# Three weight tiles at a time at the start of each inner sub-layer, and the last norm on VectorE alone

## The chip, the cores and the metric

The kernel runs on one core of one Trainium2 chip. The metric is device time in microseconds (us) of one execution. TensorE (PE) multiplies, VectorE (DVE) and ScalarE (ACT) work on its inputs and results, GpSimd (POOL) does a few adds and issues some DMAs, and SyncE (SP) issues nearly all DMAs.

## What is computed

Two layers, each a mixer sub-layer and an MLP sub-layer, on 16 meta tokens and 512 tokens of 1024 features, all in float32. Each sub-layer normalises its input and its output (`rmsnorm` divides by the root of the mean square over the 1024 features):

```python
for l in range(DEPTH):
    a = rmsnorm(h, mix_pre_g[l])
    proj = a @ w_in[l]
    ...
    y = jnp.concatenate([rmsnorm(y_attn, attn_out_g[l]),
                         rmsnorm(y_conv, conv_out_g[l])], axis=-1)
    h = h + rmsnorm(y @ w_out[l], mix_post_g[l])
    a = rmsnorm(h, mlp_pre_g[l])
    f = jnp.square(jax.nn.relu(a @ w_up[l])) @ w_down[l]
    h = h + rmsnorm(f, mlp_post_g[l])
return h[:, N_META:]
```

`proj` holds the queries, keys and values of a windowed attention with rotary positions, and three inputs of a gated convolution.

## The kernel before

**Layout.** Activations lie transposed: 128 features (a k tile, 8 in all) on the partitions, tokens along the row. The 528 tokens are worked in two halves, A of 272 (or 256, `XA`, in the second layer where the meta tokens are no longer needed) and B of 256 tokens. A float32 product is three matmuls (`mm3`, L193 to L195): weight and activation are split into a high and a low part (`whi`, `wlo`, `a_hi`, `a_lo`), and the product of the low parts is left out. So one output tile (128 features) of one half is 8 k tiles by 3, 24 matmuls, in a PSUM bank.

**Weights** come in half tiles over SP's queue. ScalarE makes `whi` (L108) and VectorE `wlo` (L109), up to `CAP` = 7 tiles ahead.

**A boundary** (`boundary`) ends a sub-layer and starts the next. TensorE multiplies the last 6 output tiles of half B while `Post` for half A (`pA`) runs beside it, k tile by k tile (`step`): `t = z * s` (L321, or L323 with a gain), `h += t` (L324), both on VectorE; `a_hi` (L330) and a square (L276) on ScalarE; the sum of squares `acc` (L277) and, one k tile later, `a_lo` (L335) on VectorE. `s` is the reciprocal root of the mean square of `z`: TensorE adds up over the partitions (`meansq`, L232), ScalarE takes three steps (L242 to L244) and VectorE two (L245, L246). Below, that is "the chain".

**`first_tiles`** then runs the first 5 output tiles (`NA`) of the next sub-layer on half A, one after another, each with its own loop over k; `mms`, which it calls, can run several items side by side, with all their matmuls of one k tile before the next. After k = 1 of the first tile, the call `pB.start` issues the mean square of half B, and between the tiles `pB.steps` issues the steps of half B, two k tiles each. In tile 2, after k = 5, stands `rstd_a`, the mean square of half A for the next norm. Then tiles 0 to 2 run side by side on half B (72 matmuls), and tiles 3 and 4. Evacuations of the results and low parts (L904, L281) run on VectorE, with ScalarE between. At the start of the kernel the same function is called with `Start` in the place of `Post` (`initial`).

There are three inner boundaries: from the first mixer to the first MLP (B0), from the first MLP to the second mixer (B1) and from the second mixer to the second MLP (B2). In B1 the five first tiles are v, k and three of q. v is scaled by its rstd (L576) and transposed on TensorE (L582); k and q are rotated on VectorE (L558 to L560, L602, L612), with DMAs that swap rows.

**The last norm** (`finish`, L342 to L359) has no next sub-layer: per k tile of 256 tokens a multiply by `s`, an add to `h`, and a store of 128 KB. Six k tiles run on VectorE with stores from SP's queue, two (`LAST_ON_POOL`) on GpSimd with stores from ScalarE's queue.

**Order.** A scheduler that replays the program on a model of the engines fixes each engine's order; the code gives only the order of issue and the data that must wait.

## Time and profile before

| | |
|---|---|
| time, median of 3 runs | 1141.37 us (1140.63 to 1142.13) |
| the profiled execution, time | 1140.6 us |
| its span | 1138.8 us |
| PE busy | 1088.9 us, 96% |
| DVE busy | 822.3 us, 72% |
| ACT busy | 641.2 us, 56% |
| POOL busy | 20.2 us, 2% |
| granted TensorE clock, mean | 0.975 of full speed |
| chain of work that ended last | PE 87%, DVE 7%, ACT 3% |
| PE idle until DVE's `acc` (L277), before L232 | 20.9 us, 9 times |
| PE idle until ACT's `a_hi` (L330) | 6.2 us |
| PE idle until DVE's `a_lo` (L335) | 4.1 us |

Busy time is the time in which an engine had an instruction in work. A PE that is busy is not one at its peak: its matmuls overlap, and their spacing, not their duration, is what one costs. The span is from the first to the last event of the trace; the execution's own time is 1.8 us more.

### The profile page before, as it was taken

How to read it: one execution, taken by the hardware profiler on the slowest of the kernel's cores; microseconds unless marked ns; L12 is line 12 of the kernel's file. 1: busy time of each engine (PE TensorE's matmuls, PEld its weight loads, DVE VectorE, ACT ScalarE, POOL GpSimd, SP SyncE). 2: the span in 40 equal slices, each digit the busy share in tenths (PEclk: the TensorE clock that was granted, in tenths of full speed). 3: DMA queues.
4: the chain of work that ended last, by engine and by line, in shares of the span. 5: the costliest groups of instructions: out<-in, count | busy, mean ns of one | idle time of the engine just before them, and what ended most of it. 6: DMA issues, size and time to landing. Idle time of an engine off the chain costs nothing.

```text
span 1138.8 us, 21453 instructions
## 1 busy us (share of the span) xinstructions
PE 1088.9 (96%) x8066; PEld 1042.9 (92%) x8066; DVE 822.3 (72%) x1941; ACT 641.2 (56%) x1542; POOL 20.2 (2%) x56
## 2 busy tenths in 40 slices
PE   8999889899999999999989997898999999999995
PEld 8999789899999999999978997898888988988995
DVE  7987867868486586586689878678855856856836
ACT  8665766655383274275456556666734734724732
POOL 3000000000000000000000000000000000000001
PEclk9999989899999999999989999898999999999998
DMA  9242122242243243144132421222422522522502
GB/s 263 66 124 65 38 75 68 81 117 70 66 131 102 61 126 112 50 119 130 43 88 59 116 63 47 66 75 75 123 81 65 148 85 65 156 77 67 147 1 75
DMA packets 197672, 102.04 MB, mean 90 GB/s; under 512 B 7424, under 2 KB 197520, under 8 KB 197568
## 3 DMA queue, kind: packets, MB, share of 16 engines
q1 hardware_dynamic: 196960, 100.15, 30.4%
q8 instruction: 63, 1.03, 0.4%
q14 instruction: 41, 0.34, 0.1%
q10 hardware_dynamic: 432, 0.32, 0.1%
q0 software_dynamic: 176, 0.21, 0.1%
HBM read 97.88 MB, written 2.10 MB: 88 GB/s over the span
## 4 chain that ended last, share of the span: by engine, by line
PE 87%; DVE 7%; ACT 3%; issue 1%; DMA 1%; SPq 0%; DVEq 0%; POOL 0%; ACTq 0%
PE ps L195 28%; PE ps L193 28%; PE ps L194 27%; PE ps L199 2%; DVE wlo L109 1%; PE ps L232 1%; ACT S L647 1%; DMA h<-in_xT 1%; DVE acc L277 1%; PE ps L693 1%; DVE p L281 1%; DVE a_lo L335 0%; DVE S L658 0%; DVE z L706 0%; DVE h L324 0%
## 5 line engine op out<-in xcount | busy, mean ns | idle before, releaser
L194 PE MATMUL ps<-f_lo,whi 128*128 128x256 f32 (+2 forms) x1072 | 326.1, 305 | 0.0
L195 PE MATMUL ps<-f_hi,wlo 128*128 128x256 f32 (+2 forms) x1072 | 325.4, 305 | 0.0
L193 PE MATMUL ps<-f_hi,whi 128*128 128x256 f32 (+2 forms) x1072 | 323.7, 306 | 0.0
L193 PE MATMUL ps<-a_hi,whi 128*128 128x256 f32 (+3 forms) x808 | 242.5, 302 | 7.2 <-ACT a_hi L330 6.2
L194 PE MATMUL ps<-a_lo,whi 128*128 128x256 f32 (+3 forms) x808 | 238.5, 295 | 4.6 <-DVE a_lo L335 4.1
L195 PE MATMUL ps<-a_hi,wlo 128*128 128x256 f32 (+3 forms) x808 | 237.1, 294 | 0.3 <-DVE wlo L109 0.3
L194 PEld LDWEIGHTS ps<-f_lo,whi 128*128 128x128 f32 x1072 | 201.7, 188 | 9.6
L195 PEld LDWEIGHTS ps<-f_hi,wlo 128*128 128x128 f32 x1072 | 201.9, 189 | 9.2
L193 PEld LDWEIGHTS ps<-f_hi,whi 128*128 128x128 f32 x1072 | 200.1, 188 | 9.3
L108 ACT ACTIVATE whi<-wraw 128x512 fp32r<-128x512 f32 x264 | 153.8, 623 | 94.2 <-PE ps L194 65.6
L109 DVE TENSOR_TENSOR wlo<-wraw,whi 128x512 fp32r<-128x512 f32 x264 | 173.1, 686 | 44.0 <-ACT whi L108 21.3
L193 PEld LDWEIGHTS ps<-a_hi,whi 128*128 128x128 f32 x808 | 157.7, 196 | 11.9 <-ACT a_hi L330 8.2
L194 PEld LDWEIGHTS ps<-a_lo,whi 128*128 128x128 f32 x808 | 158.2, 196 | 9.3 <-DVE a_lo L335 6.5
L195 PEld LDWEIGHTS ps<-a_hi,wlo 128*128 128x128 f32 x808 | 158.5, 196 | 1.8 <-DVE wlo L109 0.5
L505 DVE TENSOR_TENSOR z<-z,ps 128x272 f32<-128x272 f32 (+2 forms) x78 | 37.9, 486 | 100.3 <-PE ps L195 100.2
L194 PE MATMUL ps<-a_lo,wf 128*128 128x264 f32 (+1 forms) x384 | 108.0, 283 | 0.0
L193 PE MATMUL ps<-a_hi,wf 128*128 128x264 f32 (+1 forms) x384 | 107.8, 283 | 0.0
L108 ACT ACTIVATE wf<-wraw 128x512 fp32r<-128x512 f32 x96 | 59.7, 626 | 84.3 <-PE ps L194 51.5
L195 PE MATMUL ps<-a_hi,wf 128*128 128x264 f32 (+1 forms) x384 | 107.1, 283 | 0.0
L108 ACT ACTIVATE wf<-u 128x512 fp32r<-128x512 f32 x72 | 45.2, 628 | 87.8 <-PE ps L194 73.6
L109 DVE TENSOR_TENSOR wf<-wraw,wf 128x512 fp32r<-128x512 f32 x96 | 65.5, 686 | 10.9 <-ACT wf L108 9.8
L194 PEld LDWEIGHTS ps<-a_lo,wf 128*128 128x128 f32 x384 | 72.2, 188 | 0.1
(179 smaller groups left out, 1833.9 us busy)
## 6 DMA issues: line engine op xcount, KB each, us to landing
wraw<-in_w_up SPq DMA_DIRECT2D x128, 256.0 KB
wraw<-in_w_down SPq DMA_DIRECT2D x128, 256.0 KB
wraw<-in_w_in SPq DMA_DIRECT2D x72, 256.0 KB
wraw<-in_w_out SPq DMA_DIRECT2D x32, 128.0 KB
wraw<-in_w_out SPq DMA_DIRECT2D x16, 256.0 KB
outT<-h SPq DMA_DIRECT2D x14, 128.0 KB
h<-in_xT SPq DMA_DIRECT2D x4, 272.0 KB
h<-in_xT SPq DMA_DIRECT2D x4, 256.0 KB
```

The lines of the kernel that those rows point to most:

```text
L108: ACT.activation(hi, raw, AF.Copy)
L109: DVE.tensor_tensor(lo, raw, hi.bitcast(F32), ALU.subtract)
L193: PE.matmul(ps, whi, ahi, start=first, stop=False, skip_group_check=onto)
L194: PE.matmul(ps, whi, alo, start=False, stop=False, skip_group_check=onto)
L195: PE.matmul(ps, wlo, ahi, start=False, stop=last, skip_group_check=onto)
L199: PE.matmul(ps, a[n], b[n], start=first and n == 0, stop=last and n == 1)
L232: PE.matmul(ps, ones[:, which, :], acc, start=True, stop=more is None)
L277: return (eng or DVE).tensor_tensor(acc, acc, sq, ALU.add)
L281: DVE.tensor_tensor(lo, src, hi.bitcast(F32), ALU.subtract)
L505: DVE.tensor_tensor(zz, zz, ps, ALU.add)
L647: ACT.activation(S[:, i, keys], S[:, i, keys], AF.Exp, bias=ng[:, i:i + 1], accum_out=dn[:, i:i + 1])
L693: PE.transpose(bk[:, j * P:(j + 1) * P], S[:, j, kb * P:(kb + 1) * P], ident)
```

## The change

In `first_tiles` the first three tiles of half A are now one call of `mms` (side by side), where the sub-layer is an inner one. `pB.start` stands after k = 4 of the group, `rstd_a` after k = 5 of tile 3, and two `pB.steps` follow the group. `finish` uses VectorE only, with instructions over two k tiles and four stores of 256 KB, by turns from SP and ScalarE. The sums of squares of the start (`Start.sums`) use VectorE only, too, and the tile whose issue the five small DMAs of GpSimd wait for (`self.pool`) is another; in the built order these DMAs stand first of GpSimd's work.

```diff
-LAST_ON_POOL = (3, 6)
...
         def finish(self):
 
             t0, t1 = self.r
+            n = t1 - t0
             self.start()
-            for eng, ks, queue in ((DVE, [k for k in range(KT) if k not in LAST_ON_POOL], nc.sync), (POOL, LAST_ON_POOL, nc.scalar)):
...
+            both = self.s.unsqueeze(1).to_broadcast([P, 2, n])
+            for k in range(0, KT, 2):
+                t = utile()[:, :2 * n].rearrange("p (k t) -> p k t", k=2)
+                hk = h[:, k:k + 2, t0:t1]
+                DVE.tensor_tensor(t, z[:, k:k + 2, t0:t1], both, ALU.mult)
+                DVE.tensor_tensor(hk, hk, t, ALU.add)
+                (nc.sync, nc.scalar)[k // 2 % 2].dma_start(
+                    outT.rearrange("(k p) t -> p k t", p=P)[:, k:k + 2, t0 - NM:t1 - NM], hk)
...
-                s = add_sq("h", k == 0, h[:, k, self.r[0]:self.r[1]], self.r, DVE if k % 2 else POOL)
-                self.pool = s if k == 2 else self.pool
+                s = add_sq("h", k == 0, h[:, k, self.r[0]:self.r[1]], self.r)
+                self.pool = s if k == 3 else self.pool
...
         initial = isinstance(pB, Start)
-        at = (2, 4) if initial else (2, 5)
-        for i in range(NA):
+        at = (2, 4) if initial else (3, 5)
+        groups = [(i,) for i in range(NA)] if initial else [(0, 1, 2), (3,), (4,)]
+        steps = iter(range(4))
+        for group in groups:
+            i = group[0]
             hooks = {}
             if i == 0:
-                hooks = {1: pB.start}
+                hooks = {1 if initial else 4: pB.start}
             if i == at[0]:
                 hooks = {at[1]: rstd_a}
             if not initial:
-                evs += mms([iA[i]], act, hooks)
+                evs += mms([iA[j] for j in group], act, hooks)
...
+            ready = [evs] if initial else [evs[:3]] if i == at[0] else [[ev] for ev in evs]
             if i >= at[0]:
...
-            if i < 4:
-                pB.steps(i)
-            after(i)
+            for n in (0, 1)[:1 if len(group) == 1 else 2]:
+                m = next(steps, None)
+                if m is not None:
+                    pB.steps(m)
+            after(group[-1])
```

Line numbers shift: L193 to L195 become L192 to L194, L232 becomes L231, L324 L323 and L335 L334; behind `first_tiles` L558 becomes L560, L576 L578, L612 L614 and L904 L906.

TensorE at B0, before: the end of tile 0 on half A (`ps_2936`), the mean square of half B (`acc_2244`), and the start of tile 1 (`ps_2985`).

```order
L195 MATMUL ps_2936<-a_hi_70,wlo_2562 128x272
L193 MATMUL ps_2936<-a_hi_70,whi_2561 128x272 [waits Activation_49]
L194 MATMUL ps_2936<-a_lo_71,whi_2561 128x272 [waits DVE_49]
L195 MATMUL ps_2936<-a_hi_70,wlo_2562 128x272
L232 MATMUL ps_2944<-acc_2244,ones_86 128x256 [waits DVE_49]
L193 MATMUL ps_2985<-a_hi_70,whi_2669 128x272
L194 MATMUL ps_2985<-a_lo_71,whi_2669 128x272
```

And now: the last k tile of the group (three banks, `ps_2936` to `ps_2938`), the mean square of half B, and the start of tile 3 (`ps_3051`).

```order
L192 MATMUL ps_2936<-a_hi_70,whi_2561 128x272 [waits Activation_49]
L192 MATMUL ps_2937<-a_hi_70,whi_2669 128x272
L192 MATMUL ps_2938<-a_hi_70,whi_2721 128x272
L193 MATMUL ps_2936<-a_lo_71,whi_2561 128x272 [waits DVE_49]
L194 MATMUL ps_2936<-a_hi_70,wlo_2562 128x272
L193 MATMUL ps_2937<-a_lo_71,whi_2669 128x272
L194 MATMUL ps_2937<-a_hi_70,wlo_2670 128x272
L193 MATMUL ps_2938<-a_lo_71,whi_2721 128x272
L194 MATMUL ps_2938<-a_hi_70,wlo_2722 128x272
L231 MATMUL ps_2985<-acc_2244,ones_86 128x256 [waits DVE_49]
L192 MATMUL ps_3051<-a_hi_70,whi_2776 128x272
```

The mean square of half B stood behind 24 matmuls of half A, each k tile's three waiting by themselves for that k tile; it now stands behind 72, nine to a k tile.

VectorE at B0, before: the end of half B's steps, with the evacuations (L904) and low parts (L281) of half A's tiles among them; the last `a_lo` is the third row from the end.

```order
L324 TENSOR_TENSOR h<-h,t 128x256 [waits DVE_49]
L281 TENSOR_TENSOR f_lo<-t,f_hi 128x272 [waits Activation_49]
L321 TENSOR_TENSOR t<-z,s 128x256
L335 SCALAR_TENSOR_TENSOR a_lo<-h,gt,a_hi 128x256 [waits Activation_49]
L324 TENSOR_TENSOR h<-h,t 128x256 [waits DVE_49]
L277 TENSOR_TENSOR acc<-acc,t 128x256 [waits Activation_49]
L904 TENSOR_SCALAR t<-ps 128x272 [waits PE_49]
L335 SCALAR_TENSOR_TENSOR a_lo<-h,gt,a_hi 128x256 [waits Activation_49]
L277 TENSOR_TENSOR acc<-acc,t 128x256 [waits DVE_49,Activation_49]
L281 TENSOR_TENSOR f_lo<-t,f_hi 128x272 [waits Activation_49]
```

And now; again the third row from the end.

```order
L323 TENSOR_TENSOR h<-h,t 128x256 [waits DVE_49]
L280 TENSOR_TENSOR f_lo<-t,f_hi 128x272 [waits Activation_49] x2
L320 TENSOR_TENSOR t<-z,s 128x256
L334 SCALAR_TENSOR_TENSOR a_lo<-h,gt,a_hi 128x256 [waits Activation_49]
L276 TENSOR_TENSOR acc<-acc,t 128x256 [waits Activation_49]
L323 TENSOR_TENSOR h<-h,t 128x256 [waits DVE_49]
L334 SCALAR_TENSOR_TENSOR a_lo<-h,gt,a_hi 128x256 [waits Activation_49]
L276 TENSOR_TENSOR acc<-acc,t 128x256 [waits Activation_49]
L906 TENSOR_SCALAR t<-ps 128x256 [waits PE_49] x3
```

Up to the last `h` (L324 before, L323 now) there stand, counted from the chain's end (L246, L245), one more `acc`, one more evacuation and one more `f_lo`, three rows; and the last `a_lo` follows its `h` at once, where an `acc` and an evacuation stood between them.

VectorE at B1, before: the rotations of q (L558, L559, L560, L612) around the last steps of half B; the last `a_lo` is the tenth row.

```order
L324 TENSOR_TENSOR h<-h,t 128x256 [waits DVE_49]
L559 TENSOR_TENSOR t<-t,z 128x256 [waits DMAHW2_49,DMAHW7_49,DMAHW1_49,DMAHW0_49]
L323 SCALAR_TENSOR_TENSOR t<-z,gt,s 128x256
L612 TENSOR_TENSOR f_hi<-t,f_hi 64x256 [waits Activation_49]
L612 TENSOR_TENSOR f_lo<-t,f_lo 64x256 [waits Activation_49]
L324 TENSOR_TENSOR h<-h,t 128x256 [waits DVE_49]
L335 SCALAR_TENSOR_TENSOR a_lo<-h,gt,a_hi 128x256 [waits Activation_49]
L277 TENSOR_TENSOR acc<-acc,t 128x256 [waits Activation_49]
L558 TENSOR_TENSOR t<-z 128x256
L335 SCALAR_TENSOR_TENSOR a_lo<-h,gt,a_hi 128x256 [waits Activation_49]
L277 TENSOR_TENSOR acc<-acc,t 128x256 [waits DVE_49,Activation_49]
```

And now; the last `a_lo` is the last row.

```order
L614 TENSOR_TENSOR f_hi<-t,f_hi 64x256 [waits Activation_49]
L614 TENSOR_TENSOR f_lo<-t,f_lo 64x256 [waits Activation_49]
L562 TENSOR_TENSOR t<-t 128x256 [waits DVE_49]
L323 TENSOR_TENSOR h<-h,t 128x256 [waits DVE_49]
L561 TENSOR_TENSOR t<-t,z 128x256 [waits DMAHW5_49,DMAHW6_49,DMAHW4_49,DMAHW3_49]
L322 SCALAR_TENSOR_TENSOR t<-z,gt,s 128x256
L614 TENSOR_TENSOR f_hi<-t,f_hi 64x256 [waits Activation_49]
L614 TENSOR_TENSOR f_lo<-t,f_lo 64x256 [waits Activation_49]
L334 SCALAR_TENSOR_TENSOR a_lo<-h,gt,a_hi 128x256 [waits Activation_49]
L323 TENSOR_TENSOR h<-h,t 128x256 [waits DVE_49]
L276 TENSOR_TENSOR acc<-acc,t 128x256 [waits Activation_49]
L334 SCALAR_TENSOR_TENSOR a_lo<-h,gt,a_hi 128x256 [waits Activation_49]
```

The rotation of one more query tile (L561, L614 twice) has moved ahead of the last two `a_lo`; the low part of v's transposes (`vv`, L281), which stood ahead of the k tile before these, has moved behind it.

## Rows read from the trace of the kernel before

**Rows 1.** The page, part 4: the share of the span that each engine holds of the chain of work that ended last.

```profile
PE 87%; DVE 7%; ACT 3%; issue 1%; DMA 1%; SPq 0%; DVEq 0%; POOL 0%; ACTq 0%
```

**Rows 2.** TensorE's timeline around the boundary from the first mixer to the first MLP: start (us), duration (us), engine, line, operation, tiles, shape, count, and in brackets the idle time before it and what ended it. The rows are the first matmul of the next sub-layer on half A, the last before its first wait, one of its waits, the mean-square matmuls of half B, the first matmul of the three tiles on half B, and the mean-square matmuls behind their 72.

```profile
203.69 0.29 PE L193 MATMUL ps<-a_hi,whi 128*128 128x272 f32 x1
...
205.82 0.29 PE L195 MATMUL ps<-a_hi,wlo 128*128 128x272 f32 x1
...
208.37 0.47 PE L194 MATMUL ps<-a_lo,whi 128*128 128x272 f32 x1 [1.11 <-DVE a_lo L335]
...
212.13 1.22 PE L232 MATMUL ps<-acc,ones 128*128 128x256 f32 x2 [1.14 <-DVE acc L277]
...
226.63 0.28 PE L193 MATMUL ps<-a_hi,whi 128*128 128x256 f32 x1
...
235.16 0.59 PE L232 MATMUL ps<-acc,ones 128*128 128x256 f32 x2
```

**Rows 3.** Busy time by stretches of 4 us of the same boundary: stretch, length, then for PE, PEld, DVE, ACT and POOL the busy us and the number of instructions that start in it; then TensorE's granted clock, the DMA share and GB/s.

```profile
204.00:208.00 4.00, 2.50 (x18) 2.07 (x17) 3.63 (x10) 3.13 (x8) 0.00 (x0) 1.00 0.25 72
...
208.00:212.00 4.00, 2.05 (x5) 1.16 (x5) 3.41 (x9) 2.95 (x7) 0.00 (x0) 0.57 0.43 127
...
212.00:216.00 4.00, 3.87 (x17) 3.69 (x18) 2.36 (x6) 1.55 (x4) 0.00 (x0) 0.58 0.89 256
```

**Rows 4.** VectorE's and (213.45) ScalarE's timeline at the same boundary, columns as in rows 2: the start of the chain of half B, two `wlo` subtractions in a row, then the `h` and the low part (`a_lo`) of its last k tile, and the first evacuation after them.

```profile
213.45 0.47 ACT L242 ACTIVATE t<-ps,epst 128x256 f32<-128x256 f32 x1 [1.21 <-PE ps L232]
...
211.99 1.29 DVE L109 TENSOR_TENSOR wlo<-wraw,whi 128x512 fp32r<-128x512 f32 x2
...
228.26 0.42 DVE L324 TENSOR_TENSOR h<-h,t 128x256 f32<-128x256 f32 x1
...
229.28 0.48 DVE L335 SCALAR_TENSOR_TENSOR a_lo<-h,gt,a_hi 128x256 fp32r<-128x256 f32 x1
...
234.65 0.78 DVE L904 TENSOR_SCALAR t<-ps 128x256 f32<-128x256 f32 x2 [3.86 <-PE ps L195]
```

**Rows 5.** The boundary from the first MLP to the second mixer: TensorE's timeline (mean square of half B, the transposes of v, the mean square behind the 72 matmuls on half B), VectorE's timeline (the mixer's rstd of half A, the evacuation of v, the low part of v's transposes, the `h` of the last k tile of half B), and two stretches of busy time as in rows 3.

```profile
579.39 1.22 PE L232 MATMUL ps<-acc,ones 128*128 128x256 f32 x2 [1.15 <-DVE acc L277]
...
594.01 0.49 PE L582 MATMUL ps<-ident,u 128*128 128x128 f32 x3
...
606.64 1.06 PE L232 MATMUL ps<-acc,ones 128*128 128x256 f32 x2
...
590.03 0.44 DVE L245 SCALAR_TENSOR_TENSOR t<-ps,t 128x272 f32<-128x272 f32 x1 [0.39 <-ACT t L244]
...
592.17 0.43 DVE L576 TENSOR_TENSOR u<-ps,rt 128x272 f32<-128x272 f32 x1
...
595.07 0.56 DVE L281 TENSOR_TENSOR vv<-ps,vv 128x384 fp32r<-128x384 f32 x1 [1.40 <-ACT vv L280]
...
602.94 0.43 DVE L324 TENSOR_TENSOR h<-h,t 128x256 f32<-128x256 f32 x1
...
598.00:602.00 4.00, 2.90 (x25) 2.69 (x23) 3.90 (x10) 2.16 (x6) 0.35 (x2) 1.00 0.16 41
...
602.00:606.00 4.00, 2.81 (x15) 2.60 (x16) 3.41 (x10) 1.94 (x6) 0.00 (x0) 0.81 0.01 2
```

**Rows 6.** The boundary from the second mixer to the second MLP: TensorE (first matmul on half A, mean square of half B, mean square behind the 72 on half B), ScalarE (start of the chain of half B), VectorE (an evacuation that waits, and the `h` of the last k tile of half B).

```profile
772.11 0.28 PE L193 MATMUL ps<-a_hi,whi 128*128 128x256 f32 x1
...
780.39 1.22 PE L232 MATMUL ps<-acc,ones 128*128 128x256 f32 x2 [1.27 <-DVE acc L277]
...
803.53 0.59 PE L232 MATMUL ps<-acc,ones 128*128 128x256 f32 x2
...
781.71 0.47 ACT L242 ACTIVATE t<-ps,epst 128x256 f32<-128x256 f32 x1 [1.21 <-PE ps L232]
...
789.52 0.42 DVE L904 TENSOR_SCALAR t<-ps 128x256 f32<-128x256 f32 x1 [0.19 <-PE ps L195]
...
796.47 0.42 DVE L324 TENSOR_TENSOR h<-h,t 128x256 f32<-128x256 f32 x1
```

**Rows 7.** The last norm: TensorE's mean-square matmuls, ScalarE's first step after them, then VectorE's multiplies (L354) and adds (L358) and GpSimd's multiplies.

```profile
1126.68 0.70 PE L234 MATMUL ps<-t,ones 128*128 128x256 f32 x2 [0.53 <-ACT t L508]
...
1127.42 0.47 ACT L242 ACTIVATE t<-ps,epst 128x256 f32<-128x256 f32 x1 [0.25 <-PE ps L234]
...
1129.74 1.29 DVE L354 TENSOR_TENSOR t<-z,s 128x256 f32<-128x256 f32 x2
...
1130.95 0.94 DVE L358 TENSOR_TENSOR h<-h,t 128x256 f32<-128x256 f32 x1
...
1133.54 0.41 DVE L354 TENSOR_TENSOR t<-z,s 128x256 f32<-128x256 f32 x1
...
1135.21 0.75 DVE L358 TENSOR_TENSOR h<-h,t 128x256 f32<-128x256 f32 x2
...
1129.84 1.76 POOL L354 TENSOR_TENSOR t<-z,s 128x256 f32<-128x256 f32 x2 [469.98 <-DVE s L246]
```

**Rows 8.** The start of the kernel: from the list of waits of the first 40 us (engine, line, what it waits for: us in all, times, longest), one stretch of busy time as in rows 3, and GpSimd's first DMA issue.

```profile
DVE acc L277 <- POOL acc L277: 1.3, 2, 0.7
...
8.00:12.00 4.00, 3.26 (x14) 2.52 (x15) 3.15 (x6) 4.00 (x11) 3.04 (x5) 0.82 1.16 325
...
9.69 0.71 POOL L1035 DMA_DIRECT2D ident<-in_ident  x1
```

More of the change, by code (lines that the diff above doesn't have):

```diff
@@ L344, in finish @@
             t0, t1 = self.r
+            n = t1 - t0
             self.start()
-            for eng, ks, queue in ((DVE, [k for k in range(KT) if k not in LAST_ON_POOL], nc.sync), (POOL, LAST_ON_POOL, nc.scalar)):
-                last, ts = None, {}
-                for n in range(len(ks) + 1):
-                    with ExitStack() as es:
-                        if last is not None:
-                            es.enter_context(tc.issue_after(last.ins))
-                        if n < len(ks):
-                            ts[n] = tmp(t1 - t0)
-                            last = eng.tensor_tensor(ts[n], z[:, ks[n], t0:t1], self.s, ALU.mult)
-                    if n:
-                        k = ks[n - 1]
-                        with tc.issue_after(last.ins):
-                            last = eng.tensor_tensor(h[:, k, t0:t1], h[:, k, t0:t1], ts[n - 1], ALU.add)
-                        self.store(queue, k)
+            both = self.s.unsqueeze(1).to_broadcast([P, 2, n])
[6 more added lines that the diff above has]
+                    outT.rearrange("(k p) t -> p k t", p=P)[:, k:k + 2, t0 - NM:t1 - NM], hk)
         def flush(self):
@@ L443, in first_tiles @@
                 evs += mms([iA[i]], act, hooks)
+            ready = [evs] if initial else [evs[:3]] if i == at[0] else [[ev] for ev in evs]
             if i >= at[0]:
-                waiting = pend[:]
-                pend.clear()
-                for ev in evs:
-                    ev()
-                evs = []
-                for f in waiting:
-                    f()
-            if i < 4:
-                pB.steps(i)
-            after(i)
+                for run in ready:
+                    waiting = pend[:]
+                    pend.clear()
+                    for ev in run:
+                        ev()
+                    for f in waiting:
+                        f()
+                evs = [] if initial else evs[3:] if i == at[0] else []
+            for n in (0, 1)[:1 if len(group) == 1 else 2]:
[3 more added lines that the diff above has]
+            after(group[-1])
         cap[0] = pcap
```

## The prediction

> **What bounds the kernel now.** I read the chain of work that ended last first: PE holds 87% of it [rows 1]. So a change pays where TensorE waits or runs at its lower clock, and at the two ends, where TensorE is not the last. Next I read TensorE's timeline at the inner boundaries. At B0 the first matmul on half A starts at 203.69 and the next ones follow 0.125 us apart (17 steps to 205.82); then tile 0 waits for k tiles 6 and 7, for a high or a low part each time, 1.11 us in the row shown, and the mean square of half B starts only at 212.13, after 1.14 us for the sum of squares [rows 2]. The stretches say what that costs twice over: the granted clock is 1.00 in 204 to 208 and 0.57 and 0.58 (between the levels of 2.4 and 1.2 GHz) in 208 to 216, where 17 matmuls take 3.87 us, 0.228 each [rows 3]. Behind it TensorE runs through: the 72 matmuls of tiles 0 to 2 on half B go from 226.63 to 235.16, 0.118 each, with no wait. VectorE meanwhile is ahead: the last low part of half B starts at 229.28, and then VectorE has nothing to do for 3.86 us [rows 4]. B2 is the same picture, B1 is not: there VectorE has rotations to do, the low parts come last, and TensorE stands at 602 to 606 (15 matmuls in 4 us) [rows 5].
>
> **B0, step by step.** With three tiles side by side each k tile gives TensorE nine matmuls, 1.13 us, instead of three. Half A's last parts had all come by 210.99 (212.13 less the 1.14 of waiting), and the group needs k tile 7 after 63 matmuls, at 203.69 + 63 x 0.125 = 211.6. So the waits go, and with them the low clock. But the mean square of half B now stands behind 72 matmuls, 203.69 + 72 x 0.125 = 212.69. ScalarE's part of the chain started 1.32 us behind it at the lower clock (213.45) [rows 2, 4]; at the full clock the row of the last norm gives 0.74 (1126.68 to 1127.42) [rows 7]. 212.69 + 0.74 = 213.43: the chain starts when it started before.
>
> What is late next is therefore VectorE. From 214.85 to 230 it hardly paused before, so rows count. The new order puts three more rows ahead of the last `h`; a row costs 0.34 (the spacing of 1133.54 to 1135.21, five steps). So `h` comes at 228.26 + 3 x 0.335 = 229.26, and the last `a_lo` 1.02 behind it as before (228.26 to 229.28: ScalarE's `a_hi` lies between), done 0.48 later, at 230.76. Of half B's last nine matmuls six need it: 6 x 0.118 = 0.71. The mean square that stood at 235.16 stands at about 231.5: **3.7 us** gained. Behind these new waits on TensorE are only tiles 3 and 4 of half B, and their evacuations move forward with them. If the extra rows cost nothing it is 4.6; if ScalarE adds half a row to each of the last k tiles, 3.0.
>
> **B2.** 772.11 + 72 x 0.118 = 780.61, plus 0.74 is 781.35, where the chain started at 781.71: 0.36 earlier. An evacuation that waited 0.19 no longer does. The last `h`: 796.47 - 0.36 - 0.19 + 1.0 = 796.92; plus 1.02, 0.48 and 0.71 is 799.1, against 803.53 [rows 6]: **4.4 us**, between 3.7 and 5.4 for the same reasons.
>
> **B1.** The sum of squares decides the start of the chain (579.39) in both kernels; the full clock gives 0.58 (1.32 less 0.74). The rstd for v no longer waits 0.39, since the mean square of half A follows 18 matmuls behind. The 1.40 us for v's transposes go, because that row now stands behind eight others. Against this the new order puts six rows more ahead of the last `h`: one `a_lo`, three steps of rotation, two rotated halves of a query, about 2.3 us. The last `h` stays where it was: 602.94 - 0.58 - 0.39 - 1.40 + 2.3 = 602.9; with 1.02, 0.48 and six matmuls (0.71, or 1.4 at the lower clock) that ends at 605.1 to 605.8, against 606.64. TensorE itself gains nothing of its 5.8 us earlier end of half A: it waits for v's evacuation, now at about 591.2 (592.17 - 0.97), before the transposes [rows 5]. I take **0.8 us**, and -1.0 to 1.5 as bounds: the lower one if the rotation's DMAs or ScalarE hold the query that moved forward.
>
> **Last norm.** Before, six k tiles on VectorE and two on GpSimd. While GpSimd worked, one VectorE instruction of 256 took 0.94 us, alone 0.41, with 0.34 from start to start [rows 7]. Now eight instructions of 512. Their nearest row is the pair of `wlo` subtractions of that size: 1.29 for two, so 0.60 from start to start and 0.69 for the last [rows 4]. 1129.74 + 7 x 0.605 + 0.69 = 1134.66, against 1135.21 + 0.75 = 1135.96: 1.3 less. The last store is 256 KB instead of 128, at the 325 GB/s of row 8:12 0.4 us more [rows 8]. Together **0.85 us**; 0.3 if nothing overlaps between instructions (0.69 each), 1.3 if the store costs nothing.
> By the Trainium skill (VectorE: DVE Perf Modes, "The TRN2 errata") such an instruction pays a fixed cost each time and takes 691 ns at 512 elements; an estimate from that page is 8 x 0.691 = 5.5 us, and the sum would end 0.6 us later. The duration of the row agrees; the start of the next does not wait for it, so I keep the row.
>
> **Start.** Six adds of 0.34 us go from GpSimd to VectorE, 2.0 us, and the 1.3 us that VectorE waited for GpSimd's go away. The five small DMAs, which began at 9.69, now stand ahead of the big loads: 196 KB at 325 GB/s are 0.6 us if TensorE's first operands are behind them [rows 8]. Bounds 0.6 lost to 0.3 gained; I take **0.3 lost**, since the loads are what the start waits for.
>
> **Sum.** 3.7 + 4.4 + 0.8 + 0.85 - 0.3 = 9.45. The profiled execution took 1140.6 (its span of 1138.8 and 1.8 around it, which I leave as they are): 1131.15. It lies 0.77 under the median of 1141.37, so the forecast is **1131.9**.
>
> **Rivals.** *The clock falls in the new waits.* Half B's 72 matmuls now wait for each of the last four k tiles, about 0.7 us in 1.75. At B1 TensorE waits in the same manner: the stretch 598 to 602, busy for 2.90 of 4 us, kept a clock of 1.00, the next one, with the two longest waits, shows 0.81 [rows 5]. The new waits lie between. A fall costs what 17 matmuls lost in 212 to 216, 3.87 - 17 x 0.125 = 1.7 us [rows 3], at B0 and at B2: 1135.3.
>
> *TensorE is the bound, VectorE keeps up.* Then B0 ends at 203.69 + 120 x 0.125 + 0.5 + 72 x 0.118 = 227.7, 7.5 us gained, and B2 at 772.11 + 192 x 0.118 + 0.5 = 795.3, 8.2: 1124. Against it stands that VectorE hardly pauses there.
>
> *B1 pays* the lower bound: 1133.7.
>
> *Nothing comes of it:* the gain of half A is given back whole in half B's waits. About 1140.6 to 1141.4. That needs `h` some 4 us later than worked out.
>
> *Slower:* half B's chain now starts behind 72 matmuls. If the group ran at 0.228 each, it would take 16.4 us, end at 220.1 at B0, and the chain start at 221.4, 8.0 later than worked out, 8.5 at B2. The terms 3.7 and 4.4 become -4.3 and -4.1: 1148.4. It turns to a loss where the chain starts 4.7 us later at both, that is with 46 of the 72 at the lower clock. Against it: clock 1.00 in 204 to 208, and no wait left in the group.
>
> **How the numbers follow.** Forecast 0.50; clock 0.22; TensorE the bound 0.08; B1 pays 0.10; nothing 0.05; slower 0.05. All the better bounds together give 13.1 us (1128.3), all the worse ones 5.1 (1136.3). The range 1128 to 1136 takes in forecast, clock and B1, 0.82. Faster by over 0.2% (2.3 us, about what a measurement of this kernel can tell from no change) are the first four, 0.90; within it 0.05; slower 0.05.
>
> **What would show it.** Right: no wait in the 72 matmuls of half A, granted clock 1.00 in 204 to 216, mean square of half B near 212.7; waits for `a_lo` in half B's group, and the mean square behind it near 231.5 less what the start moved; B1 nearly unchanged in length, with TensorE idle some 6 us before v's transposes; eight instructions of 0.6 us at the end. Wrong: a clock under 1.00 behind 224 or 794, `a_lo` rows of half B without pauses and yet later, or a first real matmul over 0.6 us later than before.

## The result and the profile after

The changed kernel took 1130.86 us (median of 4 runs, 1129.28 to 1131.79), the kernel before 1141.0 (4 runs, 1140.44 to 1142.13): a ratio of 0.9903, interval 0.9884 to 0.9922. That is 10.1 us less; 9.45 was forecast. The profiled execution after is the quickest of its four (1129.28, span 1127.5), so the two traces lie 11.3 us apart.

The page, parts 2 and 4: the granted clock in 40 slices, and the shares of the chain that ended last. VectorE holds 8% of it, 7% before [rows 1]. The mean clock went from 0.975 to 0.983.

```profile
PEclk9999989999999999999999999899999999999998
...
PE 87%; DVE 8%; ACT 3%; issue 1%; DMA 1%; SPq 0%; DVEq 0%; ACTq 0%
```

**B0.** TensorE's timeline, columns as in [rows 2]: the first matmul on half A, the mean square of half B, the first of the 72 matmuls on half B, the waits among them, the mean square behind them.

```profile
202.94 0.29 PE L192 MATMUL ps<-a_hi,whi 128*128 128x272 f32 x1
...
211.97 0.59 PE L231 MATMUL ps<-acc,ones 128*128 128x256 f32 x2
...
218.86 0.51 PE L192 MATMUL ps<-a_hi,whi 128*128 128x256 f32 x3
...
223.91 0.39 PE L193 MATMUL ps<-a_lo,whi 128*128 128x256 f32 x1 [0.27 <-DVE a_lo L334]
...
225.12 0.62 PE L192 MATMUL ps<-a_hi,whi 128*128 128x256 f32 x3 [0.23 <-ACT a_hi L329]
...
229.33 0.62 PE L192 MATMUL ps<-a_hi,whi 128*128 128x256 f32 x3 [0.23 <-ACT a_hi L329]
...
230.67 0.59 PE L231 MATMUL ps<-acc,ones 128*128 128x256 f32 x2
```

Busy time by stretches, columns as in [rows 3], and VectorE's last low part of half B.

```profile
204.00:208.00 4.00, 4.00 (x34) 4.00 (x34) 3.94 (x10) 2.38 (x7) 0.00 (x0) 1.00 0.32 94
208.00:212.00 4.00, 4.00 (x34) 4.00 (x34) 3.41 (x8) 3.20 (x7) 0.00 (x0) 1.00 0.31 91
212.00:216.00 4.00, 4.00 (x32) 3.87 (x31) 2.41 (x7) 1.80 (x4) 0.00 (x0) 1.00 0.84 246
...
224.00:228.00 4.00, 3.11 (x18) 2.28 (x18) 4.00 (x13) 2.92 (x8) 0.00 (x0) 1.00 0.00 0
```

```profile
229.31 0.48 DVE L334 SCALAR_TENSOR_TENSOR a_lo<-h,gt,a_hi 128x256 fp32r<-128x256 f32 x1 [0.58 <-ACT a_hi L329]
```

Half A's group has no wait, and 61 matmuls start in 208 to 216 at clock 1.00 instead of 22 at 0.57 and 0.58 [rows 3]. (The counts in such rows are of the instructions in work in the stretch, those that began before it too.) The 72 matmuls on half B begin 15.92 us behind the first matmul instead of 22.94. The waits now sit among them, some 0.25 us each, and the clock stays at 1.00 there (224 to 228: 3.11 us busy). VectorE's low parts set the end, as worked out.

**B1.** TensorE, then VectorE, columns as in [rows 5].

```profile
587.73 0.88 PE L584 MATMUL ps<-ident,u 128*128 128x128 f32 x3 [5.99 <-DVE u L578]
...
599.27 0.62 PE L192 MATMUL ps<-a_hi,whi 128*128 128x256 f32 x3 [2.03 <-ACT a_hi L329]
600.34 0.58 PE L193 MATMUL ps<-a_lo,whi 128*128 128x256 f32 x1 [0.45 <-DVE a_lo L334]
...
603.71 0.63 PE L231 MATMUL ps<-acc,ones 128*128 128x256 f32 x2
```

```profile
585.01 0.44 DVE L244 SCALAR_TENSOR_TENSOR t<-ps,t 128x272 f32<-128x272 f32 x1 [0.39 <-ACT t L243]
...
589.51 0.44 DVE L560 TENSOR_TENSOR t<-z 128x272 f32<-128x272 f32 x1 [0.86 <-DMA z<-t]
...
595.28 0.42 DVE L560 TENSOR_TENSOR t<-z 128x256 f32<-128x256 f32 x1 [0.36 <-DMA z<-t]
...
601.20 0.48 DVE L334 SCALAR_TENSOR_TENSOR a_lo<-h,gt,a_hi 128x256 fp32r<-128x256 f32 x1 [0.24 <-ACT a_hi L329]
```

The stall of 1.40 in front of `vv` (L281 before) is gone; that of 0.39 for the rstd of v stayed; two new ones wait for the DMAs that swap rows.

To compare runs that do not begin at the same time, the table gives stages: *length* from the first matmul on half A to the mean square behind the 72 on half B; *att.* the first two intervals between mean squares in the second mixer's attention; *tail* from the last mean square of the reduction (L232, L231 after) to the end of the span. Of the stretches left out, the MLPs, the largest, take 333.91 and 322.03 us in every run; the one behind B1, up to the next mean square, takes 81.69 before, 81.14 after and 81.07 to 82.07 in e1 to e8; the others do not differ. Its 0.55 us go with the clock: the first 4 us behind B1 show 0.84 before and 0.99 after, 0.74 in e6 (82.05) and 1.00 in e1 and e2 (81.08).

| run | start to B0 | B0 | B1 | att. | B2 | tail | span |
|---|---|---|---|---|---|---|---|
| before | 203.69 | 31.47 | 37.57 | 26.36, 20.78 | 31.43 | 13.25 | 1138.8 |
| after | 202.94 | 27.73 | 39.13 | 24.65, 19.78 | 27.05 | 12.51 | 1127.5 |
| e1 | 204.74 | 27.72 | 36.84 | 26.35, 20.63 | 27.04 | 13.17 | 1130.1 |
| e2 | 202.59 | 31.48 | 39.01 | 26.36, 20.76 | 31.07 | 12.48 | 1137.4 |
| e3 | 202.44 | 26.98 | 37.52 | 26.36, 19.51 | 27.85 | 13.02 | 1128.3 |
| e4 | 202.88 | 27.73 | 38.93 | 24.63, 19.74 | 27.04 | 13.34 | 1128.0 |
| e5 | 203.61 | 31.43 | 37.60 | 26.37, 20.79 | 31.39 | 13.00 | 1138.4 |
| e6 | 202.37 | 32.81 | 38.39 | 26.36, 19.53 | 30.67 | 13.34 | 1138.1 |
| e7 | 204.17 | 26.98 | 38.70 | 24.64, 19.75 | 27.03 | 13.15 | 1128.1 |
| e8 | 202.56 | 27.47 | 39.09 | 26.35, 20.48 | 27.19 | 12.51 | 1129.3 |

Before to after, in us gained: start 0.75, B0 3.74, B1 -1.56, behind B1 0.55, attention 1.71 + 1.00, B2 4.38, tail 0.74, and 0.01 from rounding: 11.3.

### The profile page after: what moved, and what is told of

Its sections match the earlier page's. It is cut to its first block, busy times and chain, and to the rows that moved or that the text cites. A ratio compares the mean times of both kernels' runs of the same rounds, so it can differ in the third digit from the quotient of the medians.

```text
span 1127.5 us, 21429 instructions
## 1 busy us (share of the span) xinstructions
PE 1083.7 (96%) x8066; PEld 1039.0 (92%) x8066; DVE 821.8 (73%) x1943; ACT 640.3 (57%) x1542; POOL 11.1 (1%) x46
## 4 chain that ended last, share of the span: by engine, by line
PE 87%; DVE 8%; ACT 3%; issue 1%; DMA 1%; SPq 0%; DVEq 0%; ACTq 0%
PE ps L194 27%; PE ps L193 27%; PE ps L192 27%; PE ps L198 2%; DVE acc L276 1%; PE ps L231 1%; DVE a_lo L334 1%; PE ps L695 1%; DVE h L323 1%; DVE wlo L108 1%; ACT S L649 1%; DMA h<-in_xT 0%; DVE t L320 0%; DVE p L280 0%; DVE t L322 0%
## 5 line engine op out<-in xcount | busy, mean ns | idle before, releaser
L193 PE MATMUL ps<-f_lo,whi 128*128 128x256 f32 (+2 forms) x1072 | 325.9, 305 | 0.0
L194 PE MATMUL ps<-f_hi,wlo 128*128 128x256 f32 (+2 forms) x1072 | 325.0, 305 | 0.0
L192 PE MATMUL ps<-f_hi,whi 128*128 128x256 f32 (+2 forms) x1072 | 323.5, 306 | 0.0
L193 PE MATMUL ps<-a_lo,whi 128*128 128x256 f32 (+3 forms) x808 | 234.7, 293 | 2.3 <-DVE a_lo L334 2.1
L192 PE MATMUL ps<-a_hi,whi 128*128 128x256 f32 (+3 forms) x808 | 231.7, 298 | 4.5 <-ACT a_hi L329 3.4
L194 PE MATMUL ps<-a_hi,wlo 128*128 128x256 f32 (+3 forms) x808 | 233.1, 291 | 0.0
L193 PEld LDWEIGHTS ps<-f_lo,whi 128*128 128x128 f32 x1072 | 201.6, 188 | 9.6
L194 PEld LDWEIGHTS ps<-f_hi,wlo 128*128 128x128 f32 x1072 | 201.8, 189 | 9.2
L192 PEld LDWEIGHTS ps<-f_hi,whi 128*128 128x128 f32 x1072 | 200.0, 188 | 9.4
L193 PEld LDWEIGHTS ps<-a_lo,whi 128*128 128x128 f32 x808 | 156.2, 193 | 6.6 <-DVE a_lo L334 3.6
L192 PEld LDWEIGHTS ps<-a_hi,whi 128*128 128x128 f32 x808 | 152.3, 193 | 8.7 <-ACT a_hi L329 4.9
L194 PEld LDWEIGHTS ps<-a_hi,wlo 128*128 128x128 f32 x808 | 156.5, 194 | 1.4 <-DVE wlo L108 0.2
L193 PE MATMUL ps<-a_lo,wf 128*128 128x264 f32 (+1 forms) x384 | 107.9, 282 | 0.0
L192 PE MATMUL ps<-a_hi,wf 128*128 128x264 f32 (+1 forms) x384 | 107.7, 282 | 0.0
L194 PE MATMUL ps<-a_hi,wf 128*128 128x264 f32 (+1 forms) x384 | 107.1, 282 | 0.0
L193 PEld LDWEIGHTS ps<-a_lo,wf 128*128 128x128 f32 x384 | 72.2, 188 | 0.1
```

The costliest lines, as they stand in the source:

```text
L192: PE.matmul(ps, whi, ahi, start=first, stop=False, skip_group_check=onto)
L193: PE.matmul(ps, whi, alo, start=False, stop=False, skip_group_check=onto)
L194: PE.matmul(ps, wlo, ahi, start=False, stop=last, skip_group_check=onto)
```

## The experiments

Each result is the median, the number of runs, and the ratio to the kernel before on the same chip with its interval. Each diff is against the changed kernel or the one before, as named, cut to the lines that decide.

**e1, groups at the MLPs alone** (against after; B1 goes back to tile by tile):

```diff
-        groups = [(i,) for i in range(NA)] if initial else [(0, 1, 2), (3,), (4,)]
+        one = initial or norm == "c"
+        groups = [(i,) for i in range(NA)] if one else [(0, 1, 2), (3,), (4,)]
```

> Groups of three only ahead of the two MLPs (B0, B2); the second mixer starts one tile after another as before; last norm and start as in the change. Theory (each boundary pays for itself, and what the changed kernel gained inside the second mixer's attention came from another order of instructions there, which this kernel does not have): first matmul on half A to the mean square behind the 72 on half B 27.7 us at B0 (31.5 before) and 27.0 at B2 (31.4), 37.6 at B1 as before, attention stretches between mean squares 26.4 and 20.8 us as before; 3.7 + 4.4 + 1.4 for both ends: about 9.5 us faster than before. Rival (the shorter attention follows from boundaries that end earlier): attention 24.7 and 19.8 here too, some 12 us faster.

1132.01 us (6 runs), 0.9926 (0.9912 to 0.994): 8.1 us faster, where 9.5 was expected. B0 and B2 have the lengths of after to 0.01 us, B1 is 36.84. The attention has the lengths of before (26.35, 20.63), so the rival fails.

**e2, the group at the second mixer alone** (against after):

```diff
+        one = initial or norm == "z"
```

> Group of three only ahead of the second mixer (B1); both MLPs start one tile after another as before; last norm and start as in the change. Theory: B1 39.1 us long instead of 37.6, 0.6 given back behind it since the mean square there runs at the full clock, attention as before 26.4 and 20.8; with 1.4 for both ends the time is 0.4 us under before, no difference. Rival (the group at B1 is what shortens the attention behind it): attention 24.7 and 19.8, 3 us faster than before.

1140.23 us (11 runs), 0.9998 (0.9989 to 1.0007), no difference, as expected. B1 is 39.01, as in after (39.13). Together, e1 and e2 put the gain on the two MLPs. No run moves the call `pB.start` without a group.

**e3, two tiles side by side instead of three** (against after):

```diff
-        groups = [(i,) for i in range(NA)] if initial else [(0, 1, 2), (3,), (4,)]
+        groups = [(i,) for i in range(NA)] if initial else [(0, 1), (2,), (3,), (4,)]
```

> As the change, but the first group holds two tiles, then three tiles by themselves. TensorE must wait again for half A's last k tiles and for its sum of squares: about 2.5 us in all where before had 3.6 and the change 0. Theory (VectorE's rows behind the start of half B's chain decide): the chain starts at most 0.4 us apart from the change's, fewer rows stand ahead of the last low part, so B0 and B2 are 26.5 to 28.5 us long, within 1 us of the change's 27.7 and 27.0; whole time within 2.5 us of the change. Rival (the gain is the waiting of half A that goes): B0 and B2 about 30 us, some 5 us slower than the change.

1131.84 us (5 runs), 0.9918 (0.9904 to 0.9932). B0 and B2 come out at 26.98 and 27.85, although TensorE waits for half A again. TensorE's timeline and the stretches of B0:

```profile
208.38 0.53 PE L192 MATMUL ps<-a_hi,whi 128*128 128x272 f32 x2 [0.49 <-ACT a_hi L329]
210.88 0.70 PE L231 MATMUL ps<-acc,ones 128*128 128x256 f32 x2 [1.20 <-DVE acc L276]
...
220.89 0.28 PE L192 MATMUL ps<-a_hi,whi 128*128 128x256 f32 x1
...
229.41 0.59 PE L231 MATMUL ps<-acc,ones 128*128 128x256 f32 x2
```

```profile
208.00:212.00 4.00, 2.41 (x13) 1.91 (x14) 3.64 (x7) 3.31 (x8) 0.00 (x0) 1.00 0.31 92
212.00:216.00 4.00, 4.00 (x32) 3.92 (x31) 2.88 (x9) 1.86 (x6) 0.00 (x0) 1.00 0.73 202
```

At B0 the clock stays at 1.00 with 2.41 us busy in 208 to 212. At B2 of the same run, behind waits of 0.46 and 1.23, it falls:

```profile
773.73 1.22 PE L231 MATMUL ps<-acc,ones 128*128 128x256 f32 x2 [1.23 <-DVE acc L276]
```

```profile
772.00:776.00 4.00, 2.77 (x12) 2.38 (x12) 2.87 (x6) 2.73 (x8) 0.00 (x0) 0.70 0.47 136
```

B2 is 27.85 here, 0.80 longer than in after and 3.58 shorter than before. So neither a group without waits nor the full clock all through is needed. What after and e3 have and before had not is an early start of the 72 matmuls on half B: 18.45 us behind the first matmul at B0 of e3, 15.92 in after, 22.94 before. The length came as expected, but not by the mechanism that the expectation names: in e3 the 72 matmuls run without a wait, in 8.52 us, so TensorE ends the stage again, while in after VectorE's low parts do.

**e4, the groups without the other two edits** (against before):

```diff
-        for i in range(NA):
+        groups = [(i,) for i in range(NA)] if initial else [(0, 1, 2), (3,), (4,)]
+        steps = iter(range(4))
+        for group in groups:
```

> Only the groups of three; last norm and start as before. Theory: 0.75 at the start and 0.73 at the end are missing against the change, so about 9.8 us faster than before, 1.5 slower than the change; attention 24.7 and 19.8 us, since its order there is the change's but for a few rows. Rival (the start's 0.75 is chance from run to run): only 0.7 slower than the change, and the first matmul on half A at B0 near 203 as there.

1130.93 us (5 runs), 0.9916 (0.9903 to 0.9929). The attention came as expected (24.63, 19.74); the 1.5 us by which it was to be slower than the change do not show.

**e5, the last norm alone** (against before, with the rest of the new `finish`):

```diff
+            for k in range(0, KT, 2):
...
+                DVE.tensor_tensor(t, z[:, k:k + 2, t0:t1], both, ALU.mult)
+                DVE.tensor_tensor(hk, hk, t, ALU.add)
```

> Only the last norm of the change (VectorE alone, two k tiles per instruction, four stores of 256 KB). Theory: VectorE ends 1.3 us earlier behind the last mean square, the larger last store gives 0.4 to 0.9 of it back, 0.3 to 0.9 us faster than before. Rival (the stores take all of it): no difference, the tail behind the last mean square 13.25 us as before.

1141.25 us (11 runs), 0.9998 (0.9989 to 1.0008): 0.3 us faster by the medians, which is no difference from before.

**e6, the sums of squares of the start alone** (against before):

```diff
-                s = add_sq("h", k == 0, h[:, k, self.r[0]:self.r[1]], self.r, DVE if k % 2 else POOL)
-                self.pool = s if k == 2 else self.pool
+                s = add_sq("h", k == 0, h[:, k, self.r[0]:self.r[1]], self.r)
+                self.pool = s if k == 3 else self.pool
```

> Only the start's sums of squares on VectorE, with the small DMAs ahead of the loads. Theory (the start's 0.75 in the changed kernel's profile was chance: the four profiles so far put the first matmul on half A at B0 between 202.4 and 204.7): no difference from before, within 0.5 us either way. Rival (the sums gain 0.75): 0.7 us faster, first matmul near 202.9 in the median.

1139.84 us (11 runs), 0.9991 (0.9982 to 1.0): by the medians 1.7 us faster, where 0.5 either way was expected, with an interval that just reaches 1.0. So e4 to e6: the groups are the change, and neither of the other two edits can be told from nothing.

The edit touches only the start, yet B0 is 1.33 longer, B1 0.82 longer, B2 0.76 shorter. At B0 and B1 the order is not the reason: TensorE, VectorE and ScalarE have the same rows in the same order there as before. At B0 the stretch at the lower clock lies elsewhere. Before, it falls in part on TensorE's waits [rows 3]; here it begins later and falls for the most part on matmuls that run without a wait:

```profile
208.00:212.00 4.00, 2.10 (x6) 1.50 (x7) 3.67 (x7) 2.92 (x7) 0.00 (x0) 0.78 0.29 86
212.00:216.00 4.00, 4.00 (x20) 4.00 (x19) 2.40 (x7) 1.73 (x5) 0.00 (x0) 0.50 0.72 204
216.00:220.00 4.00, 4.00 (x28) 3.92 (x28) 4.00 (x12) 2.63 (x8) 0.00 (x0) 0.87 0.00 1
```

In 216 to 220 the clock was 1.00 before. The 72 matmuls on half B begin 24.28 us behind the first matmul, 1.34 later than before, and the stage ends 1.33 later.

**e7, two, one and three tiles side by side at B0, B1 and B2** (against after):

```diff
+WIDTHS = (2, 1, 3)
...
+        g = 1 if initial else WIDTHS[bound[0] - 2]
+        groups = [tuple(range(g))] + [(i,) for i in range(g, NA)]
```

> As the change, with two tiles side by side at B0, one at B1, three at B2; the built order of the second mixer's attention is that of the changed kernel but for four rows. Theory (each stretch has its own length, whatever stands ahead): B0 27.0 us, B1 36.8 to 37.6, B2 27.0, attention 24.7 and 19.8; some 2 us faster than the change, 12 faster than before. Rival (the attention is shorter only behind a group at B1): attention 26.4 and 20.8, no faster than the change.

1130.06 us (4 runs), 0.9904 (0.989 to 0.9917): no different from the change, where 2 us faster was expected. The best lengths of B0 and B2 came (26.98, 27.03) and the short attention too (24.64, 19.75), so that rival fails; but B1, tile by tile, took 38.70 where 36.8 to 37.6 was expected.

**e8, rows off VectorE between the group and half B's last low part** (against after; in the MLPs, half A's low parts are issued behind half B's first 72 matmuls, `f` waiting in `z`, and the built order puts three of them ahead of VectorE's part of half B's chain):

```diff
+            f = z[:, m, t0:t1]
+            DVE.tensor_scalar(f, ps, 0.0, None, ALU.max)
+            ACT.activation(f, f, AF.Square)
+            ACT.activation(hi, f, AF.Copy)
+            lows.append(lambda: DVE.tensor_tensor(lo, f, hi.bitcast(F32), ALU.subtract))
```

> As the change, but half A's results on the way to the MLP are evacuated into the free half of z instead of the eight shared buffers, and their low parts are issued behind the group on half B; the built order then puts the first three evacuations and low parts ahead of half B's chain on VectorE, and one evacuation fewer and four low parts fewer or more beside it. Attention order as before. Theory (VectorE's rows decide half B's end, each 0.34 us): the evacuations stand ahead of the last sum of squares and hold it until the group has ended, so the chain starts 1.5 to 2 us later, eight rows fewer behind it give 2.7 back: B0 and B2 26.5 to 27.7 us, the whole 1 to 3 us slower than the change for the attention's order. Rival (the start of the chain alone decides): B0 and B2 29.5, 7 us slower than the change.

1132.28 us (5 runs), 0.9925 (0.9911 to 0.9938). The mean square of half B came later, with a new wait:

```profile
213.42 0.70 PE L231 MATMUL ps<-acc,ones 128*128 128x256 f32 x2 [1.67 <-DVE acc L276]
...
230.04 0.59 PE L231 MATMUL ps<-acc,ones 128*128 128x256 f32 x2
```

It stands 10.86 behind the first matmul instead of 9.03 (at B2 9.99 instead of 8.52), and the stage ended 0.26 earlier at B0 and 0.14 later at B2. The end of the chain and the last `h` at B0, in after and then in e8:

```profile
214.52 0.42 DVE L245 SCALAR_TENSOR_TENSOR s<-t 128x256 f32<-128x256 f32 x1
...
228.30 0.44 DVE L323 TENSOR_TENSOR h<-h,t 128x256 f32<-128x256 f32 x1
```

```profile
216.19 0.42 DVE L245 SCALAR_TENSOR_TENSOR s<-t 128x256 f32<-128x256 f32 x1
...
227.69 0.42 DVE L323 TENSOR_TENSOR h<-h,t 128x256 f32<-128x256 f32 x1
```

From the first row to the second it is 13.78 us in after, with 38 rows between them, and 11.50 in e8, with 31: 2.28 for seven rows, 0.33 each, the price that the prediction gave a row. The chain ends 2.05 later, counted from the first matmul, and the rows taken away pay for it. So the rows on VectorE between the chain and the last `h` count as much as the start of the chain.

**e9 to e11, what holds B1** (against after, each at B1 alone). e9: the mean square of half A for v right behind k = 7 of the group. e10: all four steps of half B right behind the group. e11: both.

```diff
+            if not initial and norm == "c":
+                if i == 0:
+                    hooks[7] = rstd_a
...
-            for n in (0, 1)[:1 if len(group) == 1 else 2]:
+            for n in range(4 if len(group) == 3 and norm == "c" else 2 if len(group) == 3 else 1):
```

> As the change, but ahead of the second mixer the mean square of half A, and with it v's rstd, is issued with the last k tile of the group (its sum of squares is ready there) and no longer in tile 3. Theory (at B1 two things hold TensorE to the same end: v's evacuation, behind half B's first steps in ScalarE's order, and the last low part of half B, behind the rotations on VectorE): TensorE's 6 us of waiting before the transposes go, but the last low part comes less than 2 us earlier, so B1 is 37 to 39 us long against 39.1, B0 and B2 as in the change. Rival (v's evacuation alone holds B1): 33 us or less, 5 us faster than the change.

> As the change, but ahead of the second mixer all eight steps of half B are issued right behind the group, so the rotations come behind them on VectorE. Theory (two things hold B1): the low parts are done some 26 us into B1 instead of 37, but v's rstd and evacuation now stand behind them too, the transposes come at 28 and the 72 matmuls behind them, B1 is 37 to 39 us long. Rival (the low parts alone hold B1): 29 us or less, 10 us faster than the change.

> Both of the two edits before together: v's rstd with the last k tile of the group and all eight steps of half B right behind it. Theory (two things hold B1, and only without both it is short): v evacuated some 17 us into B1, last low part near 26, B1 27 to 29 us long, 10 us less than in the change; less the 2.7 us of the change's order in the second mixer's attention, which this build does not have: 1121 to 1125. Rival (the swap DMAs of the rotations and their tables in SP's queue hold TensorE later on): B1 short, but the stretch behind it longer by as much, near 1131.

| run | time (runs) | ratio | TensorE idle before v's transposes | B1 | from there to the next mean square |
|---|---|---|---|---|---|
| after | 1130.86 (4) | 0.9903 | 5.99 | 39.13 | 81.14 |
| e9 | 1133.35 (5) | 0.9925 (0.9912 to 0.9939) | 0.47 | 39.73 | 82.40 |
| e10 | 1129.72 (4) | 0.9895 (0.9882 to 0.9909) | 11.28 | 39.18 | 81.09 |
| e11 | 1128.15 (4) | 0.9881 (0.9866 to 0.9897) | 0.46 | 27.94 | 88.56 |

Either edit alone leaves B1 as it was, or a little longer (39.73 and 39.18, where 37 to 39 was expected). TensorE's timeline in e9, then in e10:

```profile
582.95 0.52 PE L587 MATMUL ps<-ident,u 128*128 128x128 f32 x3 [0.47 <-DVE u L581]
600.15 1.01 PE L192 MATMUL ps<-a_hi,whi 128*128 128x256 f32 x3 [9.67 <-ACT a_hi L329]
```

```profile
592.69 0.87 PE L584 MATMUL ps<-ident,u 128*128 128x128 f32 x3 [11.28 <-DVE u L578]
```

With an early rstd TensorE waits 9.67 for half B's high parts, with early steps 11.28 for v. Both together take 11.2 us off B1. But 7.4 come back behind it. SP's queue in e11 (start, duration, engine, line, what is issued), first and last rows of a run of 16 swaps, and TensorE and two stretches behind it:

```profile
594.00 0.71 SPq L558 DMA_DIRECT2D z<-t  x1
...
604.73 0.62 SPq L559 DMA_DIRECT2D z<-t  x1
605.39 2.09 SPq L162 DMA_DIRECT2D wraw<-in_w_in  x4
```

```profile
610.22 0.66 PE L587 MATMUL ps<-ident,u 128*128 128x128 f32 x2 [3.49 <-ACT whi L107]
...
606.00:610.00 4.00, 0.72 (x7) 0.52 (x5) 3.62 (x11) 3.85 (x11) 0.00 (x0) 1.00 0.77 228
610.00:614.00 4.00, 3.79 (x20) 3.82 (x21) 3.91 (x10) 2.71 (x7) 0.10 (x1) 0.57 0.19 53
```

The weight loads for the next matmuls are issued behind 16 swaps, at 605.39, and TensorE hardly works from 606 to 610 (0.72 us). B1 came as expected, the whole did not: 1128.15 lies between the theory's 1121 to 1125 and the rival's 1131. e11 is the fastest kernel of this study, 2.7 us by the medians under the change, though the two intervals overlap.

**e12, the swaps on GpSimd's queue** (e11 with one more edit, so that the weights need not stand behind them):

```diff
-                    nc.sync.dma_start(sw[b:b + 8, :], raw[b + 8:b + 16, :])
+                    POOL.dma_start(sw[b:b + 8, :], raw[b + 8:b + 16, :])
```

> As e11 (both edits ahead of the second mixer), with the rotations' swap DMAs issued by GpSimd instead of SP, in both layers. Theory (in e11 four weight loads stand behind sixteen swaps of 0.67 us each in SP's queue, and TensorE waits 5.8 us for those weights behind B1): the wait of 3.5 and 2.3 us goes, the stretch from B1's end to the next mean square is 81 to 83 us instead of 88.6, B1 28 us; 1121 to 1124, 5 us faster than e11. Rival (the rotations themselves, not the loads, are late then): a wait of the same size moves into the attention, no faster than e11; swaps that land later through GpSimd's queue would show in layer 1's rotations too.

1132.85 us (5 runs), 0.993 (0.9917 to 0.9944): slower than e11, where 5 us faster was expected. The weights did go early, 1.02 us behind the mean square that ends B1 (588.93) instead of 10.66 in e11 (594.73), but TensorE now waits elsewhere. SP's queue, then TensorE:

```profile
589.95 9.33 SPq L162 DMA_DIRECT2D wraw<-in_w_in  x10
```

```profile
600.15 0.39 PE L192 MATMUL ps<-a_hi,whi 128*128 128x256 f32 x1 [2.07 <-ACT t L553]
608.64 0.66 PE L587 MATMUL ps<-ident,u 128*128 128x128 f32 x2 [5.38 <-DVE u L581]
```

The stretch behind B1 grew from 88.56 to 95.24 (layer 0 got shorter: B0 starts at 199.38). So the weights' place in SP's queue was not all that held this stretch. The edit also changed the order in both attentions, and no run takes the two apart; what holds the stretch stays open.

## Why the prediction was right, point by point

**B0 and B2: right in mechanism and size.** 3.74 against 3.7, 4.38 against 4.4. The mean square of half B was to stand 9.00 behind the first matmul at B0 and stands 9.03 behind; the chain starts 0.69 later (estimate 0.74); the last `h` was to start 25.57 behind the first matmul and starts 25.36 behind (228.30); the mean square behind the 72 was to come at 27.8 and comes at 27.73. That VectorE's rows set the end, and at the price of 0.335 us that the prediction gave them, is backed by e8. "So the waits go, and with them the low clock" holds for three tiles, but the waits need not go: in e3 two stay, 0.49 and 1.20, and the clock is 1.00 at B0.

**B1: wrong size and sign,** 0.8 forecast, within -1.0 to 1.5, and -1.56 measured in the two traces. Three sub-steps failed. "The rstd for v no longer waits 0.39": it does, because ScalarE's three steps for it (from 583.59) stand behind half B's first four high parts though its mean square ran at 577.57. And the query rows that moved forward wait 0.86 and 0.36 for their swaps, which the lower bound named. So the last `h` stands at 600.20, 35.62 behind the first matmul instead of 33.87, where no change was forecast. And behind the last low part (done at 601.68) the mean square comes 2.03 later, at the lower clock, where six matmuls were to take 0.71 or 1.4. The 1.40 did go. How much the group costs at B1 depends on what one compares: tile by tile it took 37.57 (before), 37.60 (e5), 38.39 (e6) and 38.70 (e7), with the rows of TensorE, VectorE and ScalarE in one and the same order, and 36.84 in e1; with the group 39.13, 39.01 (e2), 38.93 (e4) and 39.09 (e8). The loss is between 0.2 and 2.3 us. Waits for swaps come without the group too: one of 1.13 in e6, one of 0.69 in e7, none before. Of the rival *B1 pays*, then, the mechanism came true; the total did not follow it, because of a term that the sum lacked.

**The missing term: the second mixer's attention,** 2.71 us shorter. No edit of the change touches it, and it follows none of them: it is there without the group at B1 (e7) and not there with that group alone (e2). The longest wait in it, for the sum of squares, fell from 7.62 to 4.11:

```profile
714.69 1.22 PE L232 MATMUL ps<-acc,ones 128*128 128x256 f32 x2 [7.62 <-DVE acc L277]
```

```profile
704.24 1.14 PE L695 MATMUL ps<-ident,S 128*128 128x128 f32 x8 [1.89 <-DVE S L655]
709.49 1.22 PE L231 MATMUL ps<-acc,ones 128*128 128x256 f32 x2 [4.11 <-DVE acc L276]
```

(the first fence is of before, the second of after). VectorE's instructions there stand in another order. In the first interval after, e4 and e11 have the same order row for row, and e7 all but the same; they show 24.65, 24.63, 24.75 and 24.64. Before, e1, e2, e3, e5, e6, e8, e9 and e12 share another, row for row, and show 26.35 to 26.37; e10 has a third and shows 23.25. That the order is the cause of these 1.71 us is read from this agreement; no run changed the order alone. (e11 has the change's order, then, which its expectation denies.) The 1.00 of the second interval goes with the clock: before, e5, e8, e12 and e6 have the same rows in the same order there and take 20.78, 20.79, 20.48, 20.02 and 19.53 at a granted clock of 0.86, 0.86, 0.87, 0.90 and 0.93; after takes 19.78 at 0.91. B1's loss and the attention's gain nearly cancel, so the total was nearer than the parts: that is luck.

**The last norm: right on VectorE, a little off in the total.** Its eight instructions, in pairs:

```profile
1119.17 1.29 DVE L350 TENSOR_TENSOR u<-z,s 128x512 f32<-128x512 f32 x2
...
1122.79 1.29 DVE L351 TENSOR_TENSOR h<-h,u 128x512 f32<-128x512 f32 x2
```

From 1119.17 to 1124.08 that is 4.91 us; 4.92 were worked out from the spacing of the row. By the 691 ns of the Trainium skill (VectorE: DVE Perf Modes, "The TRN2 errata") the estimate was 5.5; the trace agrees with it as the duration of one (0.69), but the next starts 0.60 behind. From the last add to the end of the span it takes 3.42 where it took 2.85, 0.57 more instead of 0.4. The tail went from 13.25 to 12.51, but over the traces it is 12.46 to 13.17 with the new code (11 traces, mean 12.8) and 13.25 to 13.34 with the old (3 traces): 0.5 us, where 0.85 was forecast; e5 can't tell it from nothing.

**The start: not settled.** 0.3 lost was forecast, 0.75 gained is in the two traces. But with the old sums the start takes 202.88 to 203.69 (before, e4, e5) and with the new ones 202.37 to 205.16 (after, e1 to e3, e6 to e11); the spread is wider than either figure.

**The rivals.** The clock did not fall in half B's waits (1.00 in 224 to 228), although they are longer than worked out: a k tile takes 2.10 us (225.12 to 229.33 for two), not 1.75. TensorE was not the bound there: its waits for low and high parts remained. With two tiles it is (e3). The chain was not late (212.66).

**Two sums.** The worse bounds add up to 5.4, not 5.1 (1136.0, not 1136.3), and B0 without the cost of the extra rows gains 4.7, not 4.6. Neither changes the range.

## What to carry to other kernels

Where TensorE starts on inputs that come one k tile at a time, work two or three output tiles side by side, so that each k tile brings it more matmuls; then count the rows of the engine that makes the inputs, for once TensorE is early these set the end of the stage. Two tiles were as good as three here (e3): TensorE starts later on the second half, but VectorE has three rows fewer. Where that engine has other work in the stage (B1's rotations), the same grouping pulls that work forward and can cost as much as it gives. A stage that no edit touches can move too: the second mixer's attention by 1.71 us where the scheduler chose another order, B0 by 1.33 in e6 with the same order and the lower clock elsewhere. So compare stage by stage, over several builds, and look at the order and at the granted clock of a stage before a term is called confirmed.

## What the runs showed of the hardware

Two waits of some 0.25 us for every nine matmuls left the granted clock at 1.00. In e3 waits of 0.49 and 1.20 us left it at 1.00 at B0, and waits of 0.46 and 1.23 at B2 did not (0.70 in 772 to 776). The 5.99 us without work before 587.73 was followed by half the speed. Busy time by stretches of after:

```profile
588.00:592.00 4.00, 4.00 (x20) 4.00 (x19) 3.12 (x9) 2.02 (x6) 0.00 (x0) 0.50 0.07 17
592.00:596.00 4.00, 4.00 (x30) 4.00 (x29) 3.53 (x10) 2.26 (x6) 0.00 (x0) 0.81 0.07 15
```

A clock of 0.50 is the lower of the two levels (1.2 of 2.4 GHz): 20 matmuls are in work in 4 us there, 34 in 204 to 208. Half B's matmuls start 0.213 us apart at this level and 0.118 apart at 1.00. Issuing a swap of eight rows held SP's queue for 0.62 to 0.71 us (e11) and GpSimd's for 0.50 (e12, 588.69 to 594.1): sixteen of them kept four weight loads back until 605.39.
